# Two raw groups for three behind a normalisation, and its two row passes on GpSimd

## The chip, the cores and the metric

One core of one Trainium2 chip. The metric is device time in microseconds of one execution. A profile of one execution comes with the times; all clock positions below are microseconds from the start of its span.

## What is computed

One inference step of a two-layer encoder over 256 prompt frames and 32 sample frames (288 columns in all), model width 2048. Layer 0 mixes with a gated MLP, layer 1 with retention over 8 heads; each is followed by a SwiGLU network of hidden width 5632. After every sublayer comes a residual LayerNorm, four in all:

```python
x = layer_norm(ALPHA * x + h, ln_mix_g[i], ln_mix_b[i])
x = layer_norm(ALPHA * x + swiglu(x, w_ffn_in[i], w_ffn_out[i]), ln_ffn_g[i], ln_ffn_b[i])
```

Three of the four are followed by another weight product; the change is to these three. The last writes the output.

## The kernel before

**Products.** Activations lie transposed in SBUF: 16 row blocks of 128 partitions, 288 columns each. Every float32 matrix is split into a rounded part and a rest (`hi`, `lo`; for the activations `xh`, `xl`). A *product* (function `step`) is one 128x128 weight block times one row block, in three matmuls: hi·xh (line 106), hi·xl (line 107), lo·xh (line 108). A *tile* of output sums its products in one PSUM bank: 16 of them in the stages of this case.

**Weights.** They stream from DRAM in *chunks* of 8 blocks, in the order of use: one DMA on SyncE (`raw`, 3 buffers), one cast on ScalarE (`whi`, line 427, 4 buffers), one subtraction on VectorE (`wlo`, line 428, 4 buffers). `blk` issues the preparation of chunk c+3 when chunk c begins, so the cast of a chunk can start when the chunk four before it has left its buffer, and must be done three chunks later. ScalarE and VectorE do this work in their queues among everything else, in the order that the scheduler writes; TensorE's order is the program's.

**Raw groups behind a normalisation** (class `PostNorm`, functions `start`, `correct`, `norm`). The LayerNorm is y·a + b per column (a = 1/σ, b = -µ/σ), then gain and bias per row. TensorE doesn't wait for a and b: the first tiles behind a normalisation are computed from the centred, not yet scaled rows times the gain, and two more columns (gain and bias) ride along, so such a *raw* matmul has 290 columns instead of 288, in plain column order, where an ordinary product reads its columns through `turned`. `RAW` groups of four tiles are done so, each group 64 products, its tiles two steps apart (22 steps). When a raw tile is done, `correct` repairs it with a and b (VectorE lines 395 to 397, ScalarE line 398) before it is used.

Meanwhile the true rows are made. `norm(k)` takes two row blocks: y·a and then y+b (line 384, 128x576, two passes on VectorE), then gain and bias on ScalarE (line 387, one instruction a row block). In the last raw group the rows are split into xh and xl (lines 427 and 428), a row block at each step from the sixth on, after the last raw product that reads the old xh of that block. The tiles behind the raw groups read the new xh and xl.

The three stages with raw groups: layer 0's FFN (`af_in`, from 307 us; 96 chunks lie before it), retention's input matrix (`ab_in`, from 1113 us) and layer 1's FFN (`af_in`, from 1963 us). In retention a group of raw tiles is, in turn, head 0's gate, head 0's v, and head 0's k and q; the v rows go through DRAM on GpSimd's DMA queue and come back into `vw`, which ScalarE and VectorE split (`vv`).

The last normalisation is written out by hand (`finish`): there GpSimd does three pairs of rows (line 326) with a and the mean copied to SBUF, while VectorE does others with operands in PSUM (`m`, `ap`), and line 341 does gain and bias of five row blocks on VectorE, in SBUF alone. Nothing else runs element by element on GpSimd.

Of the kernel before, what the change touches and what calls it, by code (L numbers as in the profile page):

```python
# [19 lines left out]
P = 128  # L20
D = 2048
KT = D // P
NP = 256
NS = 32
NT = NP + NS
# [11 lines left out]
LN_EPS = 1e-5  # L37
GN_EPS = 1e-6
CB = 8
RAW = 3  # L40
NBLK = KT * 32 + KT * KT + KT * 96 + 32 * KT + 2 * (KT * 2 * HT + HT * KT)
NSTATE = HEADS * CB
NCH = (NBLK + NSTATE) // CB
# [142 lines left out]
class PostNorm:  # L186
# [194 lines left out]
    def norm(self, k):  # L381
        nc, d = self.nc, self.y[:, k:k + 2, :]
        for r, op in ((self.a, ALU.mult), (self.b, ALU.add)):
            nc.vector.tensor_tensor(d, d, r.unsqueeze(1).broadcast_to([P, 2, NT]), op)
        for i in (k, k + 1):
            d = self.y[:, i, :]
            nc.scalar.activation(d, d, AF.Identity, bias=self.bias(i), scale=self.gain(i))
            if self.out is not None:
                nc.sync.dma_start(self.out[:, i, :], d)
# [11 lines left out]
    def start(self, w, ms, evac):  # L401

        core, nc = self.core, self.nc
        x = lambda k: (self.xh[:, k, :NX], self.xl[:, k, :NX])
        steps = KT + 6

        def hook(g, s):
            i = g * steps + s - 12
            if 0 <= i < 5 * KT // 2 and i % 5 == 0:
                self.norm(2 * (i // 5))  # L410
            k = s - 6
            if g == RAW - 1 and k >= 0:
                split(nc, self.xh[:, k, :NT], self.xl[:, k, :NT], self.y[:, k, :])

        for g in range(RAW):
            core.group(w, 0, list(range(KT)), ms[4 * g:4 * g + 4], x,
                       lambda m, ps: evac(m, self.correct(m, ps)), lambda s, g=g: hook(g, s))
# [8 lines left out]
def split(nc, hi, lo, f):  # L426
    nc.scalar.copy(hi, f)  # L427
    nc.vector.tensor_tensor(lo, f, hi.bitcast(F32), ALU.subtract)  # L428
# [143 lines left out]
def ffn(core, cst, x, y, lnp, layer, prev, out=None):  # L572
# [4 lines left out]
    with tc.tile_pool(name=f"ffn{layer}", bufs=1, reuse_waits="tile") as pool:  # L577
        hh = moving(pool, HH, f"hh{layer}")
        hl = moving(pool, HH, f"hl{layer}")
        for half in range(2):  # L580
# [17 lines left out]
            if half == 0:  # L598
                prev.start(f"f_in{layer}", ms, evac)
                ms = ms[4 * RAW:]  # L600
            core.tiles(f"f_in{layer}", 0, list(range(KT)), ms, xs, evac, grouped=False)
# [6 lines left out]
def retention(core, cst, x, y, lnp, prev, ins, st_p_out, st_s_out):  # L608
# [4 lines left out]
    with ExitStack() as es:  # L613
# [276 lines left out]
        for grp in range(2):  # L890
            a, b, c, d = order[4 * grp:4 * grp + 4]
            ms = sum(a + b, []) + c[0] + d[0] + c[1] + d[1]
            if grp == 0:
                prev.start("b_in", ms, evac)
                ms = ms[4 * RAW:]
            core.tiles("b_in", 0, list(range(KT)), ms, xs, evac, grouped=False)
# [132 lines left out]
```

## Time and profile before

| what | value |
|---|---|
| median of 3 runs | 2788.56 us (2786.54 to 2788.65) |
| the profiled execution | 2787.81 us |
| its span | 2786.0 us |
| mean granted TensorE clock | 0.999 |
| TensorE busy | 2773.5 us |
| VectorE, ScalarE, GpSimd busy | 1695.5, 1239.8, 141.4 us |
| matmuls of 290 columns | 576 on each of lines 106 to 108 |

The page gives busy time by engine and by group of like instructions (out <- in, count, busy us, mean ns, idle time before them and who ended it), and the chain of waits that ended last. The timeline lists an engine's instructions in order of time: start, duration, engine, line, operation, what it writes and reads, and in brackets how long the engine stood idle before it and who ended that. Matmul durations overlap; their pace is read from the starts.

### The profile page before, as it was taken

What the parts mean: (1) busy time and instruction counts of PE and PEld (TensorE: products, weight loads), DVE (VectorE), ACT (ScalarE), POOL (GpSimd) and SP (SyncE); (2) the same over time, 40 slices, a digit from 0 to 9 for tenths busy, and PEclk for the clock granted to TensorE, in tenths of its full rate; (3) what the DMA queues carried; (4) which work ended last, traced back from release to release, by engine and by line L of the source; (5) the groups of instructions that cost most, each with busy time, mean ns of one, the idle gap of its engine ahead of it and who ended that gap; (6) DMA issues with size and microseconds to landing.
All of it is one profiled execution on the core that took longest, in us unless ns stands there. A gap on an engine that the chain in (4) does not pass through costs nothing.

```text
span 2786.0 us, 51417 instructions
## 1 busy us (share of the span) xinstructions
PE 2773.5 (100%) x21574; PEld 2758.3 (99%) x21574; DVE 1695.5 (61%) x2432; ACT 1239.8 (44%) x1642; POOL 141.4 (5%) x241
## 2 busy tenths in 40 slices
PE   9999999999999999999999999999999999999998
PEld 9999999999999999999999999999999999999998
DVE  5688964445444466777765666767854455444465
ACT  5454553333343444554543444445553333334343
POOL 1100000000000000012200111200000000000001
PEclk9999999999999999999999999999999999999999
DMA  8655555555555555567765666765555555555553
GB/s 279 214 188 165 168 173 173 173 174 174 174 174 174 178 172 179 180 204 233 230 197 173 197 218 213 231 192 173 167 172 173 173 174 174 174 174 174 174 174 126
DMA packets 146584, 515.49 MB, mean 185 GB/s; under 512 B 18016, under 2 KB 20336, under 8 KB 146320
## 3 DMA queue, kind: packets, MB, share of 16 engines
q1 hardware_dynamic: 131984, 473.47, 52.0%
q0 software_dynamic: 14224, 38.59, 4.6%
q8 instruction: 168, 2.75, 0.4%
q14 instruction: 64, 0.52, 0.1%
q10 hardware_dynamic: 144, 0.15, 0.0%
HBM read 486.98 MB, written 25.17 MB: 184 GB/s over the span
## 4 chain that ended last, share of the span: by engine, by line
PE 97%; DMA 1%; DVE 1%; ACT 0%; issue 0%; SPq 0%; POOL 0%; DVEq 0%; ACTq 0%; POOLq 0%
PE af_in L107 13%; PE af_in L108 13%; PE af_in L106 13%; PE ab_in L106 7%; PE ab_in L107 7%; PE ab_in L108 7%; PE af_out L106 6%; PE af_out L107 6%; PE af_out L108 6%; PE ab_out L106 2%; PE ab_out L107 2%; PE ab_out L108 2%; PE aa_in L106 2%; PE aa_in L108 2%; PE aa_in L107 2%; PE aa_out L106 1%
## 5 line engine op out<-in xcount | busy, mean ns | idle before, releaser
L428 DVE TENSOR_TENSOR wlo<-raw,whi 128x1024 fp32r<-128x1024 f32 (+1 forms) x892 | 1085.8, 1219 | 867.0 <-ACT whi L427 862.6
L427 ACT CAST whi<-raw 128x1024 fp32r<-128x1024 f32 (+1 forms) x892 | 931.8, 1046 | 1379.0 <-PE af_in L107 330.3
L107 PE MATMUL af_in<-xl,whi 128*128 128x288 f32 (+1 forms) x2816 | 815.8, 290 | 0.0
L108 PE MATMUL af_in<-xh,wlo 128*128 128x288 f32 (+1 forms) x2816 | 814.7, 289 | 0.0
L106 PE MATMUL af_in<-xh,whi 128*128 128x288 f32 (+1 forms) x2816 | 814.7, 289 | 0.0
L107 PEld LDWEIGHTS af_in<-xl,whi 128*128 128x128 f32 x2816 | 528.5, 188 | 0.0
L106 PEld LDWEIGHTS af_in<-xh,whi 128*128 128x128 f32 x2816 | 528.5, 188 | 0.0
L108 PEld LDWEIGHTS af_in<-xh,wlo 128*128 128x128 f32 x2816 | 528.4, 188 | 0.0
L106 PE MATMUL ab_in<-xh,whi 128*128 128x288 f32 (+1 forms) x1536 | 445.4, 290 | 0.0
L107 PE MATMUL ab_in<-xl,whi 128*128 128x288 f32 (+1 forms) x1536 | 444.9, 290 | 0.3
L108 PE MATMUL ab_in<-xh,wlo 128*128 128x288 f32 (+1 forms) x1536 | 444.8, 290 | 0.0
L108 PE MATMUL af_out<-hh,wlo 128*128 128x288 f32 x1408 | 406.3, 289 | 0.0
L106 PE MATMUL af_out<-hh,whi 128*128 128x288 f32 x1408 | 406.3, 289 | 0.0
L107 PE MATMUL af_out<-hl,whi 128*128 128x288 f32 x1408 | 406.3, 289 | 0.0
L107 PEld LDWEIGHTS ab_in<-xl,whi 128*128 128x128 f32 x1536 | 288.4, 188 | 1.7 <-DVE xl L428 0.7
L106 PEld LDWEIGHTS ab_in<-xh,whi 128*128 128x128 f32 x1536 | 288.4, 188 | 1.1
L108 PEld LDWEIGHTS ab_in<-xh,wlo 128*128 128x128 f32 x1536 | 288.3, 188 | 0.0
L106 PEld LDWEIGHTS af_out<-hh,whi 128*128 128x128 f32 x1408 | 264.0, 187 | 0.0
L107 PEld LDWEIGHTS af_out<-hl,whi 128*128 128x128 f32 x1408 | 264.0, 187 | 0.0
L108 PEld LDWEIGHTS af_out<-hh,wlo 128*128 128x128 f32 x1408 | 264.0, 187 | 0.0
L106 PE MATMUL aa_in<-xh,whi 128*128 128x288 f32 x512 | 148.5, 290 | 0.4 <-ACT vg L484 0.4
L108 PE MATMUL aa_in<-xh,wlo 128*128 128x288 f32 x512 | 147.9, 289 | 0.0
(249 smaller groups left out, 2909.9 us busy)
## 6 DMA issues: line engine op xcount, KB each, us to landing
raw<-in_wpack_dram SPq DMA_DIRECT2D x887, 512.0 KB, 3.4
v_room<-tv POOLq DMA_DIRECT2D x32, 144.0 KB, 5.0
of<-o_room POOLq DMA_DIRECT2D x32, 144.0 KB, 4.5
vw<-v_room POOLq DMA_DIRECT2D x8, 512.0 KB, 5.7
out_st_s_dram<-sso POOLq DMA_DIRECT2D x16, 256.0 KB, 2.8
o_room<-to POOLq DMA_DIRECT2D x8, 512.0 KB, 3.9
out_st_p_dram<-so POOLq DMA_DIRECT2D x16, 256.0 KB, 5.4
y<-in_xT_dram SPq DMA_DIRECT2D x8, 288.0 KB, 4.9
```

The source lines that it names most:

```text
L106: mm(ps, hi, xh, start=first, stop=False)
L107: mm(ps, hi, xl, start=False, stop=False)
L108: mm(ps, lo, xh, start=False, stop=last)
L427: nc.scalar.copy(hi, f)
L428: nc.vector.tensor_tensor(lo, f, hi.bitcast(F32), ALU.subtract)
```

## The change

`RAW` falls from 3 to 2: the third group's four tiles of each stage become ordinary tiles behind the raw ones. `norm` issues its two passes on GpSimd. In `hook`, a pair of rows is issued every four steps instead of every five, so that eight pairs fit into two groups, and the splits of x come in the second group.

```diff
-RAW = 3
+RAW = 2
...
         for r, op in ((self.a, ALU.mult), (self.b, ALU.add)):
-            nc.vector.tensor_tensor(d, d, r.unsqueeze(1).broadcast_to([P, 2, NT]), op)
+            nc.gpsimd.tensor_tensor(d, d, r.unsqueeze(1).broadcast_to([P, 2, NT]), op)
...
             i = g * steps + s - 12
-            if 0 <= i < 5 * KT // 2 and i % 5 == 0:
-                self.norm(2 * (i // 5))
+            if 0 <= i < 2 * KT and i % 4 == 0:
+                self.norm(i // 2)
```

How the instructions stand on three engines, in the first stage. The numbers behind names only tell buffers apart: `whi_3840` and `wlo_3841` belong to the stage's chunk 8, `whi_3870` to chunk 9, `whi_3918` (before) and `whi_3922` (changed) to chunk 10, `whi_3971` and `whi_3975` to chunk 11.

ScalarE's queue before, from chunk 8's cast on:

```order
L427 CAST whi_3840<-raw_3839 128x1024
L387 ACTIVATE y<-y,lnv 128x288 x2
L427 CAST whi_3870<-raw_3869 128x1024
L387 ACTIVATE y<-y,lnv 128x288 x2
L398 ACTIVATE fix_0_3879<-fix_0_3879,wgb_0_3878 128x288
L427 CAST whi_3918<-raw_3917 128x1024
L586 ACT_TABLE_LOAD
L586 ACTIVATE sg_0_3884<-fix_0_3879 128x288
L398 ACTIVATE fix_0_3908<-fix_0_3908,wgb_44_3907 128x288
L427 CAST whi_3971<-raw_3970 128x1024
```

and after the change:

```order
L427 CAST whi_3840<-raw_3839 128x1024
L387 ACTIVATE y<-y,lnv 128x288 x5
L427 CAST whi_3870<-raw_3869 128x1024
L387 ACTIVATE y<-y,lnv 128x288
L398 ACTIVATE fix_0_3879<-fix_0_3879,wgb_0_3878 128x288
L387 ACTIVATE y<-y,lnv 128x288
L586 ACT_TABLE_LOAD
L586 ACTIVATE sg_0_3884<-fix_0_3879 128x288
L427 CAST whi_3922<-raw_3921 128x1024
L398 ACTIVATE fix_0_3912<-fix_0_3912,wgb_44_3911 128x288
L387 ACTIVATE y<-y,lnv 128x288 x2
L427 CAST whi_3975<-raw_3974 128x1024
```

Five instructions of line 387, not two, now stand between the casts of chunks 8 and 9; the fifth belongs to the third pair of rows.

GpSimd's queue after the change, between the clearing of the sums for the next normalisation and retention's first DMA; before, nothing stood between those two:

```order
L233 MEMSET sums_11077 128x576
L384 ISA
L384 TENSOR_TENSOR y<-y,a_3728 128x576 x4
L384 TENSOR_TENSOR y<-y,b_3729 128x576 x4
L384 TENSOR_TENSOR y<-y,a_3728 128x576 x2
L384 TENSOR_TENSOR y<-y,b_3729 128x576 x2
L384 TENSOR_TENSOR y<-y,a_3728 128x576 x2
L384 TENSOR_TENSOR y<-y,b_3729 128x576 x2
L623 DMA r_cs<-in_rope_dram 128x576
```

The sixteen passes stand in a row; the third pair's b pass is the seventh, the seventh pair's the fifteenth.

VectorE's queue after the change, from chunk 9's lo half to chunk 11's (before, the passes of line 384 stood among these rows):

```order
L428 TENSOR_TENSOR wlo_3871<-raw_3869,whi_3870 128x1024
L395 COPY wgb_44_3911<-af_in_44_48_3674 128x2
L396 TENSOR_TENSOR fix_0_3912<-af_in_44_48_3674,a_3728 128x288
L397 SCALAR_TENSOR_TENSOR fix_0_3912<-b_3729,wgb_44_3911,fix_0_3912 128x288
L395 COPY wgb_1_3942<-af_in_1_48_3690 128x2
L396 TENSOR_TENSOR fix_0_3943<-af_in_1_48_3690,a_3728 128x288
L428 TENSOR_TENSOR wlo_3923<-raw_3921,whi_3922 128x1024
L592 TENSOR_TENSOR hf_0_3917<-fix_0_3912,sg_0_3884 128x288
L397 SCALAR_TENSOR_TENSOR fix_0_3943<-b_3729,wgb_1_3942,fix_0_3943 128x288
```

It goes on with L395 and L396, the split of hf (`hl`, line 428), one more L397, and chunk 11's lo half (`wlo_3976`). What has moved is that line 384 is gone from here; of the rest, lines 395 and 396 read PSUM, and the others read SBUF alone.

## The prediction

> **What bounds the kernel now.** I read the page first: how busy each engine is, and which engine the chain of waits runs through.
>
> ```profile
> span 2786.0 us, 51417 instructions
> PE 2773.5 (100%) x21574; PEld 2758.3 (99%) x21574; DVE 1695.5 (61%) x2432; ACT 1239.8 (44%) x1642; POOL 141.4 (5%) x241
> PE 97%; DMA 1%; DVE 1%; ACT 0%; issue 0%; SPq 0%; POOL 0%; DVEq 0%; ACTq 0%; POOLq 0%
> ```
>
> TensorE never rests, so time falls only where a matmul gets cheaper or a wait of TensorE goes, and rises wherever TensorE is made to wait. The profiled execution took 2787.81 us, its span plus 1.8; the median of the runs shown, 2788.56, lies 0.75 above it. I sum against 2787.81.
>
> The timeline of TensorE gives the pace of the two kinds of product. First two rows of a stage with raw tiles, 50 products (150 matmuls) apart; then two rows of an ordinary stage, 12 products (36 matmuls) apart.
>
> ```profile
> 1124.43 0.29 PE L106 MATMUL ab_in<-xh,whi 128*128 128x290 f32 x1
> 1144.42 0.30 PE L106 MATMUL ab_in<-xh,whi 128*128 128x290 f32 x1
> ...
> 2099.80 0.29 PE L106 MATMUL af_in<-xh,whi 128*128 128x288 f32 x1
> 2104.36 0.29 PE L106 MATMUL af_in<-xh,whi 128*128 128x288 f32 x1
> ```
>
> A raw matmul takes 19.99/150 = 133.3 ns, an ordinary one 4.56/36 = 126.7 ns: the difference is 6.6 ns.
>
> **What is removed.** Each of three normalisations loses a group of 4 tiles x 16 products x 3 = 192 raw matmuls to the ordinary form: 576 x 6.6 ns = **3.8 us gained**. The corrections of twelve tiles (L395 to L398) go with it, and 48 passes leave VectorE; both engines have idle time, so I count nothing for that by itself.
>
> One wait of TensorE can go too. The timelines of TensorE and VectorE in the retention stage, where the first tile after the raw ones begins:
>
> ```profile
> 1195.38 0.29 PE L106 MATMUL ab_in<-xh,whi 128*128 128x288 f32 x1
> 1195.79 0.40 PE L107 MATMUL ab_in<-xl,whi 128*128 128x288 f32 x1
> 1196.03 0.29 PE L108 MATMUL ab_in<-xh,wlo 128*128 128x288 f32 x1
> 1196.16 0.29 PE L106 MATMUL ab_in<-xh,whi 128*128 128x288 f32 x1
> 1196.59 0.40 PE L107 MATMUL ab_in<-xl,whi 128*128 128x288 f32 x1
> 1196.83 0.29 PE L108 MATMUL ab_in<-xh,wlo 128*128 128x288 f32 x1
> ...
> 1195.28 0.46 DVE L428 TENSOR_TENSOR xl<-y,xh 128x288 fp32r<-128x288 f32 x1
> 1196.08 0.46 DVE L428 TENSOR_TENSOR xl<-y,xh 128x288 fp32r<-128x288 f32 x1
> ```
>
> The steps 0.41, 0.24, 0.43 and 0.24 stand where 0.127 is normal: 0.8 us lost to the last two splits of x. The splits now stand one raw group earlier, in front of the head's v rows and no longer behind them. I count the **0.8 us as gained**, with bounds 0 and 0.8.
>
> **What is moved, and its price.** VectorE's passes (L384) and GpSimd's for the same shape, from the groups, and GpSimd's last stretch from its timeline:
>
> ```profile
> L384 DVE TENSOR_TENSOR y<-y,a 128x576 f32<-128x576 f32 x24 | 17.4, 752 | 0.0
> L326 POOL TENSOR_TENSOR y<-y,b 128x576 f32<-128x576 f32 x3 | 4.1, 1403 | 17.0 <-ACT b L348 17.0
> ...
> 2771.47 4.14 POOL L326 TENSOR_TENSOR y<-y,b 128x576 f32<-128x576 f32 x3 [17.00 <-ACT b L348]
> 2775.57 4.13 POOL L326 TENSOR_TENSOR y<-y,a 128x576 f32<-128x576 f32 x3
> ```
>
> One pass goes from 0.75 to 4.14/3 = 1.38 us. In the changed order nothing in GpSimd's queue ties a pair to a product: 16 passes stand in a row (four a, four b, then two and two), 22.1 us, and ScalarE's L387 waits for the b pass of its pair. ScalarE is also the engine that casts the weights. Their due times, from ScalarE's and VectorE's timelines in the first stage:
>
> ```profile
> 320.22 1.06 ACT L427 CAST whi<-raw 128x1024 fp32r<-128x1024 f32 x1 [2.10 <-PE af_in L107]
> 323.32 1.05 ACT L427 CAST whi<-raw 128x1024 fp32r<-128x1024 f32 x1 [2.05 <-PE af_in L107]
> 325.36 1.15 ACT L387 ACTIVATE y<-y,lnv 128x288 f32<-128x288 f32 x2 [0.98 <-DVE y L384]
> 326.52 1.05 ACT L427 CAST whi<-raw 128x1024 fp32r<-128x1024 f32 x1
> ...
> 321.36 0.46 DVE L183 SCALAR_TENSOR_TENSOR a<-t,a 128x288 f32<-128x288 f32 x1
> 321.73 1.22 DVE L428 TENSOR_TENSOR wlo<-raw,whi 128x1024 fp32r<-128x1024 f32 x1
> ```
>
> The cast at 323.32 is chunk 8 of the stage, released when chunk 4 left its buffer. So chunk 5 begins at 323.4, and with 24 x 133.3 ns = 3.2 us each, chunk 9 begins at 336.2, chunk 11 at 342.6, chunk 12 at 345.8; the lo half is due 0.27 us later, at the third matmul. In the kernel before, chunk 9 was cast at 326.52. Now five L387 stand before it (ScalarE's order in the section on the change), the fifth behind the third b pass, GpSimd's seventh.
>
> *If GpSimd runs at 1.38 us:* it starts when a is there, 321.8; the seventh pass ends at 331.5; half a pair of L387 (1.15/2), the cast (1.05) and the lo half (1.22) put chunk 9 at 334.3, due 336.5. The tightest place is the last stage, where chunk 12's cast stands behind the fifteenth pass: 342.5 + 0.57 + 1.05 + 1.22 = 345.3, due 346.1. TensorE then waits nowhere, by 0.8 us.
>
> *What the trace says on both engines at once.* Their only common stretch is the last one, where VectorE's groups and the chain of waits show:
>
> ```profile
> L326 DVE TENSOR_TENSOR y<-y,m 128x576 f32<-128x576 f32 x3 | 2.2, 746 | 0.0
> L326 DVE TENSOR_TENSOR y<-y,ap 128x576 f32<-128x576 f32 x3 | 2.2, 747 | 0.0
> ...
> L341 DVE TENSOR_SCALAR y<-y,lnv x5: 420/421/830, 2779.0 to 2780.8; 128x288 f32<-128x288 f32 x5
> ...
> 2779.04 0.83 DVE y L341
> ```
>
> Passes with one operand in PSUM (m, ap) cost 0.75 as ever while GpSimd works. But the first L341, which reads and writes SBUF alone, took 0.83 where its fellows took 0.42: it began at 2779.04, GpSimd's last pass ended at 2775.57 + 4.13 = 2779.70, and it ended at 2779.87, as if it had got going 0.25 us before the pass ended. So some SBUF-only work of VectorE does not run beside a GpSimd pass. Whether a TENSOR_TENSOR with two SBUF operands is of that sort, no row shows. The ends are no exclusion (0 us) and full exclusion. I take exclusion, since the instructions in question (both operands and the result in SBUF) are nearer to L341 than to L326, with the handover 0.25 us before the end in either direction.
>
> [...]
>
> **The walk with exclusion.** VectorE's two-input work in the stage, from the groups:
>
> ```profile
> L428 DVE TENSOR_TENSOR wlo<-raw,whi 128x1024 fp32r<-128x1024 f32 x886 | 1082.9, 1224 | 861.8 <-ACT whi L427 857.5
> L397 DVE SCALAR_TENSOR_TENSOR fix<-b,wgb,fix 128x288 f32<-128x288 f32 x36 | 18.5, 513 | 0.1
> L592 DVE TENSOR_TENSOR hf<-fix,sg 128x288 f32<-128x288 f32 x12 | 5.5, 455 | 1.2 <-ACT fix L398 1.2
> L428 DVE TENSOR_TENSOR hl<-hf,hh 128x288 fp32r<-128x288 f32 x88 | 39.8, 452 | 0.1
> ```
>
> GpSimd's first pass waits for the lo half at 321.73 and starts at 322.7. Up to chunk 9's lo half nine passes (12.4) and two VectorE instructions (chunk 8's lo 1.22, one L397 0.51) alternate with five handovers (-1.25): that lo half starts at 335.6 and ends at 336.8, 0.3 late. From there to chunk 11's lo half VectorE has eight such instructions in a row (three lo, three L397, hf, hl: 6.1 us), and each lets one of the seven passes left go first (9.7), with 14 handovers (-3.5): 335.6 + 6.1 + 9.7 - 3.5 = 347.9, due 342.9. **5.0 us of waiting** in the first stage. In the retention stage the same row holds six instructions (5.2 us, five passes 6.9, ten handovers -2.5): 345.2, 2.3 late. In the last stage seven (5.6, 8.3, -3.0): 346.5, 3.6 late. Behind this ScalarE cannot catch up, as the busy time of the second raw group and the copies to xh show:
>
> ```profile
> core 0: us, PE busy (x) PEld busy (x) DVE busy (x) ACT busy (x) POOL busy (x), PEclk, DMA share, GB/s
> 333.05:358.65 25.60, 25.60 (x197) 25.60 (x196) 22.19 (x39) 18.65 (x32) 0.00 (x0) 1.00 0.52 168
> ...
> L427 ACT CAST xh<-y 128x288 fp32r<-128x288 f32 x64 | 26.1, 429 | 10.9 <-PE af_in L108 4.9 <-DMA y<-in_xT_dram 4.8 <-PE ab_in L108 1.3
> ```
>
> To its 18.65 of 25.6 us the sixteen copies to xh now come (0.43 each, 6.9 us): it is full. For casts and splits that stay late there I add 1 us a stage, an estimate between nothing and one such cast with its lo half (1.05 + 1.22). Together 5.0 + 2.3 + 3.6 + 3 = **14 us lost**. With no time saved at handovers the lo halves come 10.0, 6.3 and 8.1 late: 27 with the same 3. If GpSimd never lets VectorE in between passes, chunk 8's lo half, due 333.3, waits for 322.95 + 22.1 = 345.0 and ends at 346.2: 12.9 a stage, 39.
>
> **Sum.** 2787.8 - 3.8 - 0.8 + 14 = **2797 us**. With bounds: 2783 without exclusion, 2811 with slow handovers, 2822 where GpSimd keeps VectorE out.
>
> **The rivals.**
> *No exclusion, not slower: 2783 us.* For it: L326 at 0.75 beside GpSimd, and 0.8 us to spare at the tightest place. Against it: L341, and that none of the L326 reads two SBUF operands. It decides at a pass of 1.38 + 0.8/15 = 1.43 us; above it the last stage waits 15 times the excess. Chance 0.22.
> *GpSimd keeps the port: 2822 us.* For it: its passes stand back to back in its queue with 4.14 us for three, no gap. Against: they have no wait that would keep VectorE's older request behind. Chance 0.12.
> *Cheap alternation: 2786 to 2791 us.* Only part of an instruction excludes the other, and the due times swallow most. Chance 0.10.
> *The change doesn't do what it says.* The count of 48 products paces nothing, as the order shows: passes run as soon as a and b are there. This is in the walk; if the ScalarE order alone decided, the time would be that of the first rival.
> *Alternation, 2793 to 2811 us, likeliest 2797:* 0.56.
>
> **How the numbers follow.** A measurement of this kernel can tell about 0.2% (5.6 us) from no change. Slower by more, above 2794.1: nearly all of the alternation and GpSimd keeping the port, 0.68. Faster by more, below 2783.0: the first rival comes out right at this edge, 4.6 us below the profiled execution, so I give faster 0.11, and within 0.21 (the other half of it and the cheap alternation). The range reaches from the first rival to GpSimd keeping the port, 2782 to 2822; outside lie the lower half of the first and the upper part of the last.
>
> **What would show it.** Right: VectorE's L428 (lo half) and L397 with a mean over 1.3 and 0.6 us inside the stages, GpSimd passes longer than 1.40 or with gaps between them, and waits of TensorE for the lo half near chunks 9 to 12 of each stage, some 5 us in the first. Wrong: L428 at 1.22 there, GpSimd at 1.38 a pass done by 344 us, and TensorE without a wait. Raw matmuls (128x290) must fall from 384 + 192 = 576 on each of lines 106 to 108 to 384; if ordinary tiles right behind a raw group run at 133 ns as well, the 3.8 us is wrong.

## The result, and the profile after

| what | before | changed |
|---|---|---|
| median | 2788.55 us of 6 runs | 2809.32 us of 6 runs (2807.08 to 2813.79) |
| ratio | 1 | 1.0075, 95% interval 1.0057 to 1.0094 |
| the profiled execution | 2787.81 us | 2809.54 us |
| mean granted TensorE clock | 0.999 | 0.995 |

The change makes the kernel 0.75% slower: some 21 us by the medians, where the prediction said 8.4 (2797). The page and TensorE's waits of the changed kernel:

```profile
PE 2780.3 (99%) x21574; PEld 2764.2 (98%) x21574; DVE 1679.2 (60%) x2348; ACT 1233.2 (44%) x1630; POOL 225.3 (8%) x289
PE 96%; DVE 2%; POOL 1%; issue 1%; ACT 0%; DVEq 0%; POOLq 0%
```

```profile
PE af_in L106 <- DVE fix L396: 7.9, 2, 4.1
PE ab_in L106 <- DVE fix L396: 3.9, 1, 3.9
PE af_in L106 <- DVE wgb L395: 2.5, 1, 2.5
...
PE af_in L108 <- DVE wlo L428: 0.8, 1, 0.8
```

The columns are the total wait, how often, and the longest. 15.1 us in five waits, all of them in the second raw group of a stage. But only the last is for a lo half, which the prediction had put in all of them. The others are for line 396 or 395, and these release something: TensorE's product is the first of a tile, and the PSUM bank that it needs is still being read by the correction of a tile of the first group.

TensorE's timeline at this place in the first stage:

```profile
333.44 0.29 PE L108 MATMUL af_in<-xh,wlo 128*128 128x290 f32 x1
337.83 0.58 PE L106 MATMUL af_in<-xh,whi 128*128 128x290 f32 x1 [4.10 <-DVE fix L396]
338.21 0.45 PE L107 MATMUL af_in<-xl,whi 128*128 128x290 f32 x1
338.45 0.45 PE L108 MATMUL af_in<-xh,wlo 128*128 128x290 f32 x1
...
343.52 0.35 PE L108 MATMUL af_in<-xh,wlo 128*128 128x290 f32 x1
343.71 0.30 PE L106 MATMUL af_in<-xh,whi 128*128 128x290 f32 x1
...
350.03 0.40 PE L108 MATMUL af_in<-xh,wlo 128*128 128x290 f32 x1 [0.78 <-DVE wlo L428]
```

Read the starts: behind the wait they are 0.24 us apart, not 0.133, until 343.5. The same stretch by windows, with the granted clock (PEclk) in the third column from the end:

```profile
core 0: us, PE busy (x) PEld busy (x) DVE busy (x) ACT busy (x) POOL busy (x), PEclk, DMA share, GB/s
...
334.00:337.80 3.80, 0.00 (x0) 0.00 (x0) 2.69 (x4) 3.78 (x6) 3.80 (x3) 0.87 0.00 0
...
339.00:341.00 2.00, 2.00 (x10) 2.00 (x10) 2.00 (x2) 2.00 (x5) 2.00 (x2) 0.50 0.35 139
...
343.60:346.00 2.40, 2.40 (x20) 2.40 (x20) 2.40 (x5) 1.39 (x3) 2.40 (x3) 1.00 0.08 32
```

The first window lies inside the wait: 0.87 over 3.80 us is half the clock in its last 1.0 us. So TensorE was granted half its clock from 336.8 us on, before the wait of 4.10 us ended, until 343.6: 6.8 us, of which it worked 5.8. The slow matmuls count as TensorE's busy time (2.00 of 2.00 us in the window from 339 on), so the page's 99% hides it. Against the regular pace the starts lose 8.1, 6.6 and 10.3 us in the three stages, 25.0 in all: 15 as waits, some 10 as slow matmuls.

Who is late? GpSimd's groups and its timeline in the first stage:

```profile
L384 POOL TENSOR_TENSOR y<-y,a 128x576 f32<-128x576 f32 x24 | 44.1, 1863 | 24.4 <-DVE a L183 24.4
L384 POOL TENSOR_TENSOR y<-y,b 128x576 f32<-128x576 f32 x24 | 40.7, 1720 | 0.0
```

```profile
329.24 5.57 POOL L384 TENSOR_TENSOR y<-y,b 128x576 f32<-128x576 f32 x4
...
342.43 3.24 POOL L384 TENSOR_TENSOR y<-y,a 128x576 f32<-128x576 f32 x2
```

From 329.24 four passes take 1.39 us each; VectorE stands idle beside them. From 342.43 each takes 1.62, beside VectorE instructions of 0.45 to 0.51. VectorE's timeline:

```profile
335.08 2.17 DVE L428 TENSOR_TENSOR wlo<-raw,whi 128x1024 fp32r<-128x1024 f32 x1 [7.08 <-ACT whi L427]
337.18 0.15 DVE L395 COPY wgb<-af_in 128x2 f32<-128x2 f32 x1
337.25 0.44 DVE L396 TENSOR_TENSOR fix<-af_in,a 128x288 f32<-128x288 f32 x1
...
341.12 1.67 DVE L592 TENSOR_TENSOR hf<-fix,sg 128x288 f32<-128x288 f32 x1
342.71 1.67 DVE L397 SCALAR_TENSOR_TENSOR fix<-b,wgb,fix 128x288 f32<-128x288 f32 x1
...
347.52 2.45 DVE L428 TENSOR_TENSOR wlo<-raw,whi 128x1024 fp32r<-128x1024 f32 x1
```

Instructions with two operands in SBUF are too long, by 1.2 us where they wait for nearly a whole pass: L592 1.67 for 0.46, L428 2.45 for 1.22. The lo half at 335.08 came in the middle of a pass and took 0.95 too long. L395 and L396, which read PSUM, keep their 0.15 and 0.44. The tile that L396 reads was complete at about 329.4 (an estimate: seven products behind the first tile, whose L395 started at 326.69), and TensorE was ready for its bank at 333.7. But L396 stands in VectorE's queue behind the lo half of chunk 9, which waited 7.08 us for its cast on ScalarE; ScalarE in turn stood behind GpSimd:

```profile
333.48 0.63 ACT L387 ACTIVATE y<-y,lnv 128x288 f32<-128x288 f32 x1 [0.24 <-POOL y L384]
334.02 1.03 ACT L427 CAST whi<-raw 128x1024 fp32r<-128x1024 f32 x1
```

The raw matmuls fell as they should, to 256 + 128 = 384 a line:

```profile
L106 PE MATMUL af_in<-xh,whi 128*128 128x290 f32 x256 | 78.9, 308 | 10.5 <-DVE fix L396 7.9 <-DVE wgb L395 2.5
L106 PE MATMUL ab_in<-xh,whi 128*128 128x290 f32 x128 | 39.1, 305 | 3.9 <-DVE fix L396 3.9
```

### The profile page after: what moved, and what is told of

Read it like the earlier page. It is cut to its first block, busy times and chain, and to the rows that moved or that the text cites. A ratio compares the mean times of both kernels' runs of the same rounds, so it can differ in the third digit from the quotient of the medians.

```text
span 2807.4 us, 51382 instructions
## 1 busy us (share of the span) xinstructions
PE 2780.3 (99%) x21574; PEld 2764.2 (98%) x21574; DVE 1679.2 (60%) x2348; ACT 1233.2 (44%) x1630; POOL 225.3 (8%) x289
## 4 chain that ended last, share of the span: by engine, by line
PE 96%; DVE 2%; POOL 1%; issue 1%; ACT 0%; DVEq 0%; POOLq 0%
PE af_in L106 12%; PE af_in L108 12%; PE af_in L107 12%; PE ab_in L106 7%; PE ab_in L107 7%; PE ab_in L108 7%; PE af_out L108 6%; PE af_out L107 6%; PE af_out L106 6%; PE aa_in L106 2%; PE aa_in L108 2%; PE ab_out L106 2%; PE aa_in L107 2%; PE ab_out L107 2%; PE ab_out L108 2%; POOL y L384 1%
## 5 line engine op out<-in xcount | busy, mean ns | idle before, releaser
L428 DVE TENSOR_TENSOR wlo<-raw,whi 128x1024 fp32r<-128x1024 f32 (+1 forms) x892 | 1098.4, 1233 | 904.0 <-ACT whi L427 900.4
```

## The experiments

The theory after the result: GpSimd's passes and VectorE's two-input instructions take turns, VectorE falls behind in the second raw group, and TensorE waits for whatever of VectorE's comes due first. Its rivals: the two groups themselves are too few; the chain from GpSimd over ScalarE to the casts is late without any turns; the bank is a bottleneck of its own; the halved clock is a cost of its own.

### The two halves of the change apart

Two raw groups, the passes on VectorE:

```diff
-            nc.gpsimd.tensor_tensor(d, d, r.unsqueeze(1).broadcast_to([P, 2, NT]), op)
+            nc.vector.tensor_tensor(d, d, r.unsqueeze(1).broadcast_to([P, 2, NT]), op)
```

> Two raw groups as in the changed kernel, but the two passes of the normalisation back on VectorE. Theory (GpSimd's passes hold up VectorE's two-input instructions, so the corrections of the first raw group come late, TensorE waits for a PSUM bank and runs at half clock behind the wait): without GpSimd's passes only the gains are left, 576 x 6.6 ns and 0.8 us, so 2788.6 - 4.6 = 2784 us (2782 to 2787), ratio about 0.9984, granted clock 0.999 as before, lo halves at 1.22 us everywhere, no TensorE wait over 1 us on L396. Rival (two groups alone are the cause: sixteen splits of x and the corrections in fewer products crowd ScalarE and VectorE): the waits on L396 stay, 2800 us or more. If raw matmuls were no dearer than ordinary ones: 2788.

Measured: 2783.36 us (11 runs) beside 2787.24 of the kernel before, ratio 0.9985 (0.9976 to 0.9994). Its page's first row and its waits:

```profile
PE 2769.2 (100%) x21574; PEld 2754.4 (99%) x21574; DVE 1684.8 (61%) x2396; ACT 1233.4 (44%) x1630; POOL 141.4 (5%) x241
```

```profile
PE warm L924 <- POOL g_nrm L476: 1.0, 1, 1.0
PE aa_in L106 <- ACT vg L484: 0.4, 1, 0.4
```

No wait for L396 or a lo half is left, and TensorE's busy time is 4.3 us below the kernel before. The groups are not the cause; they bring the gain that was forecast for them. This is the version that beats both kernels, the one before by 0.15%.

Three raw groups, the passes on GpSimd (the edit above the other way round, in the kernel before):

> Three raw groups and a pair every 60 products as in the kernel before, but the two passes on GpSimd: that part of the change alone. Theory of contention: the waits at the second raw group are those of the changed kernel (about 25 us in three stages, wait and slow clock together), without its 4.6 us of gain: 2788.6 + 25 = 2813 us (2805 to 2818); a GpSimd pass takes 1.6 to 1.9 us in the mean and L428 is over 2 us in these stretches. Rival (the grouping is the cause and GpSimd is harmless): 2788 to 2790 us. Since the third group stands between the passes and the splits of x, up to 5 us less than 2813 would mean that the splits of x had a part in it.

Measured: 2811.63, 2813.56, 2845.09 and 2846.06 us, ratio 1.0149 (1.0098 to 1.0201) over the four. The waits of the execution at 2811.63:

```profile
PE af_in L106 <- DVE fix L396: 8.8, 3, 4.1
PE ab_in L106 <- DVE fix L396: 4.9, 2, 3.9
PE af_in L106 <- DVE wgb L395: 1.6, 1, 1.6
```

The same waits as in the changed kernel; this execution takes 24 us more than the kernel before. So GpSimd's part alone does the damage. What the two executions at 2845 did isn't known; the kernel was run twice more to see it in a trace:

> The three-group kernel with the passes on GpSimd once more, to see in a trace where its times of 2845 us (two of four executions) came from, 33 us above the other two. If GpSimd keeps VectorE out for a whole stretch of passes in some executions, L428 has instances of 8 us or more in a stage and the time is 2840 or more. If the turns always alternate, 2811 to 2814 and the 33 us must come from elsewhere.

> The same kernel a third time, for the same question: either 2811 to 2814 us with the turns as before, or 2840 and more with a stretch in the trace that shows where 33 us went.

They took 2810.81 and 2811.30 us. The 33 us stay open; one execution of the run with extra matmuls below shows them too (2846.81).

### Turns without a dependence, and a dependence without turns

Now the passes are back on VectorE, and GpSimd does the same kind of pass on a tile that nobody reads:

```diff
...
+        e = self.s
+        for r in (self.a, self.b):
+            nc.gpsimd.tensor_tensor(e, e, r.unsqueeze(1).broadcast_to([P, 2, NT]), ALU.mult)
```

> The two raw groups with the passes on VectorE (2783 us), and beside them, for each pair, two GpSimd passes of the same shape that read and write a scratch tile in SBUF which nobody uses: no instruction of another engine waits for a result of GpSimd. It leaves nothing out. Theory of exclusion (a GpSimd pass and a VectorE instruction with two SBUF inputs take turns, whatever the data): sixteen passes in a stage hold VectorE, whose own sixteen passes now take turns as well, for 16 x (1.38 - 0.24) = 18 us, of which about 6 are VectorE's slack, so some 12 us late in each stage and TensorE waits: about 2783 + 36 = 2819 (2800 to 2830), L428 in these stretches over 2 us. Rival (the loss came from the chain GpSimd, ScalarE's L387, casts, and not from the port): no result is waited for, so 2783 to 2785.

Measured: 2828.28 us, ratio 1.0150 (1.0135 to 1.0165). VectorE's timeline in the first stage:

```profile
334.66 2.45 DVE L431 TENSOR_TENSOR wlo<-raw,whi 128x1024 fp32r<-128x1024 f32 x1
337.04 1.98 DVE L384 TENSOR_TENSOR y<-y,b 128x576 f32<-128x576 f32 x1
338.94 1.95 DVE L384 TENSOR_TENSOR y<-y,a 128x576 f32<-128x576 f32 x1
```

No instruction waits for a result of GpSimd, and yet the lo half takes 2.45 and a pass 1.98 for 0.75. Turns alone cost 45 us (2828.28 - 2783.36) when VectorE has sixteen more two-input instructions to offer.

The same with memsets (one tiny pass of 4 columns, once in each normalisation, makes the first of them wait for a):

```diff
...
+        for _ in range(5):
+            nc.gpsimd.memset(e, 0.0)
```

> As the last one, but the scratch work of GpSimd is five memsets of the same tile for each pair: it writes SBUF and reads none. Theory (it is reading that takes turns with VectorE, or at least a two-operand operation): L428 stays at 1.22 and TensorE waits nowhere: 2783 to 2785. Rival (any GpSimd work in SBUF holds VectorE up): lo halves over 1.5 us beside the memsets and 2790 or more.

Measured: 2783.34 us, ratio 0.9985 (0.9975 to 0.9994). GpSimd's and VectorE's groups over the whole execution:

```profile
L389 POOL MEMSET sums<- 128x576 f32 x120 | 69.8, 582 | 6.9
...
L433 DVE TENSOR_TENSOR wlo<-raw,whi 128x1024 fp32r<-128x1024 f32 (+1 forms) x892 | 1085.7, 1219 | 879.8 <-ACT whi L432 875.2
```

70 us of GpSimd work that writes SBUF without reading it cost nothing: the lo halves keep 1.22 us, and the time is that of the two groups alone, 2783.36. So it isn't any GpSimd work in SBUF that holds VectorE up.

Between the two, a pass that reads one operand:

```diff
...
+        for _ in range(2):
+            nc.gpsimd.tensor_scalar(e, e, 0.5, None, ALU.mult)
```

> As the run with two reading scratch passes for each pair, but each of them multiplies the scratch tile by a number: one operand in SBUF in place of two, result in SBUF. It leaves nothing out. If any GpSimd instruction that reads SBUF takes turns with VectorE's two-input instructions: waits of TensorE as with two operands, scaled by the length of a pass; 2795 or more, L428 over 1.5 us beside it. If two operands are needed on GpSimd too: 2783 to 2785 as with the memsets. The evidence so far is the changed kernel's VectorE, where an instruction with one operand in SBUF (L341, 0.83 in place of 0.42 us) also waited, which favours the first.

Measured: 2795.00 us, ratio 1.0026 (1.0017 to 1.0036). VectorE in the first stage:

```profile
341.49 0.91 DVE L433 TENSOR_TENSOR hl<-hf,hh 128x288 fp32r<-128x288 f32 x1
342.32 1.21 DVE L433 TENSOR_TENSOR wlo<-raw,whi 128x1024 fp32r<-128x1024 f32 x1
343.46 1.22 DVE L384 TENSOR_TENSOR y<-y,b 128x576 f32<-128x576 f32 x1
```

One operand is enough, but the hold is at most 0.47 us in these rows (hl 0.91 for 0.45, L384 1.22 for 0.75), though GpSimd's instruction lasts 2.03 us in the mean. The lo halves keep 1.22 us in the mean (1219 ns over the whole execution, as beside the memsets). The time came out at the edge of what was expected; that L428 would be over 1.5 us was wrong in the mean, and why the lo halves go all but free isn't known.

Then the dependence alone. GpSimd still writes y for L387, but by memsets:

```diff
-            nc.gpsimd.tensor_tensor(d, d, r.unsqueeze(1).broadcast_to([P, 2, NT]), op)
+            nc.gpsimd.tensor_tensor(d[:, :, :4], d[:, :, :4], r[:, :4].unsqueeze(1).broadcast_to([P, 2, 4]), op)
+            nc.gpsimd.memset(d, 0.5)
+            nc.gpsimd.memset(d, 0.25)
```

> The changed kernel with each GpSimd pass replaced by a tiny pass of 4 columns and two memsets of the pair: GpSimd still writes y for ScalarE's L387, later than VectorE would, but reads almost nothing. It leaves out the multiplying and shifting of y by a and b (y becomes a constant there), so its output is another. Theory of exclusion: L428 and L397 stay near 1.22 and 0.51, and TensorE waits at most a microsecond or so in a stage where ScalarE's casts stand behind GpSimd: 2784 to 2788. Rival (the chain from GpSimd through L387 to the casts is the loss): waits of about 4 us at the second raw group stay, 2795 or more. The order on ScalarE may differ from that of the changed kernel, which blurs this one.

Measured: 2783.74 us, ratio 0.9987 (0.9978 to 0.9997). But only two L387 stood ahead of chunk 9's cast, where the changed kernel has five; so the tiny pass was moved between the memsets, which makes it four:

> As the last gating kernel, with the tiny pass between the two memsets of the pair: now four L387 (not two) stand ahead of ScalarE's cast of chunk 9 and four behind it, close to the changed kernel's five and two, and GpSimd's work for a pass is about 1.36 us as the undisturbed pass was. It leaves out the multiplying and shifting by a and b. Theory A (turns between GpSimd and VectorE are the whole loss): no wait over 1.5 us at the second raw group and 2783 to 2788 us, with the cast of chunk 9 some 4 us later than in the kernel before. Theory B (the late cast behind GpSimd's passes is a large part of the loss in itself): waits for the bank of 3 us or more in each stage and 2795 or more.

Measured: 2787.14 us, ratio 0.9999 (0.9989 to 1.0008). TensorE's waits:

```profile
PE af_in L106 <- DVE wgb L397: 1.5, 1, 1.5
PE ab_in L106 <- DVE fix L398: 1.2, 1, 1.2
PE af_in L106 <- ACT sg L588: 1.1, 1, 1.1
```

One wait of over a microsecond in each stage, 3.8 us in all, in the second raw group again. (The third row is in the first stage; a correction of a tile there, L398, ended at 336.75, just before TensorE went on at 336.89.) 2787.14 - 2783.36 = 3.8 us of the change's 26 (2809.32 - 2783.36) are the chain in this version, some 22 the turns. The split is rough: four is not five, and chunk 9's cast starts at 329.08 here, at 334.02 in the changed kernel. An estimate from the changed kernel's rows for five, without turns: the seventh pass would end at 321.58 + 7 x 1.39 = 331.3, and L387, the cast, the lo half and L396 behind it (0.63, 1.03, 1.22, 0.44) at 334.6, 0.9 us after TensorE is ready for the bank. That is of the same size.

### The bank and the clock

The changed kernel with the second raw group in other PSUM banks:

```diff
-                        ps[m] = (self.accum if j < 4 else self.bank)(f"a{w}_{m}_{self.ticks}")
+                        ps[m] = (self.accum if j < 4 and not spare else self.bank)(f"a{w}_{m}_{self.ticks}")
...
-                       lambda m, ps: evac(m, self.correct(m, ps)), lambda s, g=g: hook(g, s))
+                       lambda m, ps: evac(m, self.correct(m, ps)), lambda s, g=g: hook(g, s), spare=g == 1)
```

> The changed kernel with the second raw group accumulating in other PSUM banks (the ones that the small products use), which nobody has to release there. Theory A (late lo halves of the weights are what sets the end; the bank is only the first thing that is late): the waits of about 4 us on L396 go, TensorE waits for the lo halves of chunks 9 to 11 instead, 7.4 + 4.2 + 5.7 = 17 us late as the changed kernel's VectorE has them, less what no longer waits behind slow products: 2799 to 2807 us, 3 to 10 below the changed kernel. Theory B (the bank wait is the cause by itself): TensorE waits nowhere over 1 us, 2786 to 2790. Theory C (nothing changes since the corrections are late anyway): 2809.

Measured: 2808.83 us, ratio 1.0076 (1.0060 to 1.0091): no gain. The waits:

```profile
PE af_in L108 <- DVE wlo L428: 12.3, 6, 5.3
PE ab_in L108 <- DVE wlo L428: 3.8, 3, 2.1
```

The bank is free, and TensorE waits for the lo halves, 16.1 us, just where the prediction had seen it. By stage it is 7.2, 3.8 and 5.1 us. Around the last of these waits in each stage (5.3, 2.1 and 3.4 us) the clock halves as well (starts 0.24 us apart from 350.98, 1163.84 and 2018.45 on; mean clock 0.995), so that the time comes out as of theory C although the mechanism is that of A: whichever is due first shows the wait, and VectorE's delay sets the end. That the times agree so closely is in part chance: compared product by product, TensorE falls behind by 1.9 us more than in the changed kernel in the first stage, and by 2.6 us less in the last.

The changed kernel with 30 more matmuls ahead of the product that waits for the bank:

```diff
+            if g == 1 and s == 1:
+                w = self.core.bank(f"fill{self.gi}")
+                for _ in range(30):
+                    nc.tensor.matmul(w[:, :NT], self.cst["one_r"], self.xh[:, 0, :NT], start=True, stop=True)
```

> The changed kernel with 30 extra matmuls of 128 x 288 in each of the three stages (their result goes to a spare PSUM bank and is not used), put in TensorE's queue just ahead of the product that waits for the bank. They are about 30 x 0.127 = 3.8 us of work, as long as the wait. Theory (an idle stretch of about 4 us halves the granted clock for the next 5.7 us): the extra work lies inside the wait, the clock stays at 1.00, and the slow products of 6.6 and 10.3 - 6.4 us less waits go where the lo halves are not late themselves: about 3 us in the second and up to 5 in the third stage, little in the first, so 2801 to 2806 us with MORE work for TensorE. Rival (the slow products have another cause, such as the port or memory): the extra work costs nothing or up to 3 us, 2809 to 2813, and the 0.50 clock stays.

Measured: 2809.78, 2811.02, 2811.20 and the 2846.81 named above, ratio 1.0116 (1.0067 to 1.0164); the mean clock rose from 0.995 to 0.998. The extra work and two windows behind it in the first stage:

```profile
332.62 4.11 PE L414 MATMUL fill<-xh,one_r 128*128 128x288 f32 x30
336.56 0.30 PE L106 MATMUL af_in<-xh,whi 128*128 128x290 f32 x1
```

```profile
337.00:344.00 7.00, 5.09 (x37) 4.77 (x36) 6.96 (x9) 4.67 (x9) 7.00 (x5) 1.00 0.45 152
344.00:350.00 6.00, 4.52 (x32) 4.32 (x33) 5.83 (x5) 3.03 (x7) 4.38 (x3) 1.00 0.00 0
```

The clock is 1.00 here (in the last stage 3.4 us at half remain), VectorE busy for 6.96 of 7.00 us, and TensorE for 5.09: it waits at full clock for what it had before reached slowly. The profiled execution takes 0.24 us more than the changed kernel's with 11.8 us more work (3 x 3.94). So the expected 3 to 8 us did not come in the sum. But ScalarE's order is not the changed kernel's: chunk 12's cast stands behind six more L387 and starts at 352.29 in the first stage, not at 348.08, and TensorE waits 1.4 us for it and its lo half. Compared product by product, TensorE falls behind by 2.0 and 1.4 us more than in the changed kernel in the first two stages, and by 2.5 us less in the last. So in the first two the slow matmuls mostly filled a time in which VectorE was late anyway; in the last they may have been a cost of their own, and this run does not settle it.

### Half the passes

The first four pairs on VectorE, the last four on GpSimd:

```diff
-            nc.gpsimd.tensor_tensor(d, d, r.unsqueeze(1).broadcast_to([P, 2, NT]), op)
+            e = nc.vector if k < 8 else nc.gpsimd
+            e.tensor_tensor(d, d, r.unsqueeze(1).broadcast_to([P, 2, NT]), op)
```

> The changed kernel with the first four pairs of each normalisation on VectorE and the last four on GpSimd: half the passes. Theory (the turns on VectorE add up until the last lo half in the second raw group, about 8 us late in each stage with sixteen GpSimd passes): eight passes fewer take 8 x (1.38 - 0.24) = 9 us of turns away and put 8 x 0.75 = 6 us of ordinary VectorE work, early, in their place; the lateness falls from 8 to about 5 at worst and about 0 at best: 2784 to 2797, likeliest 2788. Rival (already the first passes make TensorE stop, and the stop costs about the same however short): 2803 to 2809.

Measured: 2806.59 us, ratio 1.0070 (1.0055 to 1.0085), as the rival had it. GpSimd's passes in the first stage, and one of VectorE's:

```profile
321.35 8.05 POOL L385 TENSOR_TENSOR y<-y,a 128x576 f32<-128x576 f32 x4 [7.68 <-DVE a L183]
329.36 8.06 POOL L385 TENSOR_TENSOR y<-y,b 128x576 f32<-128x576 f32 x4
...
330.40 1.98 DVE L385 TENSOR_TENSOR y<-y,b 128x576 f32<-128x576 f32 x1
```

All eight passes take 2.0 us: each meets an instruction of VectorE, whose own passes are now there to meet. In the changed kernel the four from 329.24 ran beside an idle VectorE and took no turn. My expectation counted passes; what counts is the meetings, and these hardly fell. Beside their durations without GpSimd's passes, VectorE's instructions are 9.0 us too long in the first stage here; in the changed kernel it was 9.1 there, and 7.0 and 8.7 us in the other two. That a first stop costs the same however short, as the rival put it, isn't shown by it.

## Why the prediction was right, and where it was wrong

**Exclusion** was right. L341's 0.83 us carried the choice between the two ends, and the scratch runs show it without any dependence: two operands read 2828, memsets 2783. L341 reads one tile in SBUF and L428 two, so the step from the one to the other was an analogy, which came out.

**The gain** of two groups was right: 4.6 us forecast, about 4.2 measured (0.15%; 1.7 to 6.7 by the interval), with 384 raw matmuls a line and the wait for the last splits of x gone.

**The handover is the step that failed in size.** "With the handover 0.25 us before the end in either direction" makes 0.5 us a turn. Measured: L592, 0.46 alone, starts 1.59 us ahead of the next one; 0.46 + 1.39 - 1.59 = 0.26 us are saved a turn, half of it. The walk without any saving gave 10.0, 6.3 and 8.1 us of lateness (its own terms add up to 9.7, 6.0 and 7.8), with 0.5 it gave 5.0, 2.3 and 3.6; halfway is 7.4, 4.2 and 5.7, and with the other banks TensorE waited 7.2, 3.8 and 5.1 us for the lo halves. So 10.9 us should have been 16 to 17.

**The tail was wrong in kind.** "1 us a stage" stood for casts and splits that stay late behind chunk 11. There the changed kernel's TensorE waits no more: its last wait in each stage ends at 350.03, 1150.99 and 2010.30 us. Instead 26 - 16 = 10 us are left in place of 3, and they lie ahead of that place, as matmuls at half clock. With the clock held up, part of them shows as waits for VectorE and ScalarE. How much of the 10 us the clock costs by itself stays open. That 2809 lies so near the prediction's bound of 2811 is chance: that bound adds 24 us of late lo halves and 3 of tail, and the runs show 16 and 10.

**The place was wrong, at no cost in the sum.** I walked to the lo halves and overlooked that L396, queued behind one of them, frees the bank of the next tile: that comes due first. With other banks the time was the same.

**Rivals.** "No exclusion, 2783 us, TensorE waits nowhere" missed the same bank: with the dependence kept, four L387 ahead of the cast and the turns gone, TensorE waited 1.1 to 1.5 us a stage, 2787 (with two ahead, 2784). "GpSimd keeps the port" did not happen: the longest lo half of the changed kernel takes 2.45 us, 1.23 more than alone and less than one pass of 1.39. (What the port is, at which the two engines would take turns, no run shows; the runs show the turns.) "Cheap alternation" failed on the turn, up to 1.2 us for each.

**The halved clock** was in no step. The length of a single wait doesn't tell when it comes. With half the passes there are stretches of matmuls 0.24 us apart in all three stages, and no wait there exceeds 3.3 us; with the other banks such a stretch of 3.4 us begins 1.3 us behind a wait of 2.12 us in the second stage; in the run with extra matmuls the clock stayed at 1.00 around a wait of 2.18 us in the first.

## What to carry to other kernels

Before a pass goes to GpSimd, list what VectorE does beside it with two SBUF operands: each meeting cost VectorE up to 1.2 us of the pass's 1.4 here, so price the meetings in VectorE's queue and not GpSimd's idle time. Then follow VectorE's lateness to everything in the queue behind it, the instructions that free PSUM banks too, and take the earliest due time for the wait. Before repairing the wait that the profile names, ask what is late right behind it: here other banks, and a clock held up by extra work, moved the wait and, in the sum of the stages, not the end.

## What the runs showed of the hardware

GpSimd's memsets in SBUF, 70 us of them beside VectorE's two-input work, held up nothing (lo halves 1.22 us, 2783.34 us in all). A GpSimd instruction with one SBUF operand held VectorE by up to 0.47 us at a time in the first stage, one with two operands by up to 1.2 us. The first lasted 2.03 us in the mean beside VectorE's work; the second 1.39 undisturbed, and 1.6 beside VectorE's short instructions to 2.4 beside a lo half.

In the changed kernel's trace the granted clock was 1.00 or 0.50. Its half stretches lasted 6.8 us (twice) and 10.2 us in the three stages; in the last stage of the run with extra matmuls it was 3.4 us (an estimate from its windows, 0.89 over 6.00 us and 0.66 over 3.00).
